# Up projections of the last ConvFFN in Strassen's form for the second token half, with pw2 put ahead of a down group

## The chip, the cores and the metric

One Trainium2 chip, one NeuronCore of it. The metric is the device time of one launch in microseconds. The engines are PE (matmul; its weight loads are listed as PEld), DVE (elementwise, reads SBUF and PSUM), ACT (activations and copies), POOL (elementwise, SBUF alone) and SP (issues DMAs). Each engine works through its own queue in order.

## The reference, cut to what matters

A decoder trunk of two layers runs over 16 meta tokens, 1024 prompt tokens and 8 samples of 4 tokens (1072 in all), with 1024 features in float32. Layer 0 mixes with an S5 scan and a short convolution, layer 1 with a Conformer convolution module; behind each stands a ConvFFN. The change lies in layer 1:

```
x = x + silu(layer_norm(dwconv31(v))) @ w_pw2 + b_pw2        # end of the mixer
xn = rms_norm(x) * g                                         # one factor per token
a, g = split(xn @ w_up)                                      # 2 x 2816 features
x = x + (silu(dwconv3(a)) * g) @ w_down
y = rms_norm(x) * g_final
```

`dwconv3` is causal over the tokens of the prompt and of each sample, and its last inputs are outputs too.

## The kernel before

Features lie on the 128 partitions, tokens along a row. The 1072 tokens are two halves: half 0 has 512 (in layer 1 only 496 or 498 of them are computed, since the meta tokens' results are not wanted), half 1 has 560 (528 of the prompt and 32 of the samples) and runs in two blocks of 280 columns. A residual tile `x` (`xres`) of 128 features by one half stays in SBUF: eight for each half.

Every float32 product is made of three in the `fp32r` type: both operands are split into a high part (`wh`, `xnh`, `hh`: a copy by ACT) and a rest (`wl`, `xnl`, `hl`: a subtraction, on DVE or POOL), and PE adds up high x high, high x rest and rest x high in a PSUM bank (L143, in `dense`). A weight tile of 128x1024 comes by DMA into one of two `raw` buffers (L110), and its parts go into a ring of three `wh`/`wl` pairs. POOL takes the subtraction for a share of the weights, DVE for the others (`weight`).

ConvFFN: 22 tiles `f` of 128 features. `up(f, hf)` computes tile `a` (8 K tiles x 3 parts x 2 blocks = 48 matmuls in half 1), multiplies it by the norm's factor `rstd` while it leaves PSUM (`ap`), runs the convolution over it (`c`: one step on ACT, two on DVE), then computes tile `g` in the same way; `s = silu(c) * g` (POOL) is split into `hh` and `hl`. `down(fs, ...)` multiplies a group of 4 tiles (one group has 2) with `w_down` and adds the result to the eight `x`. `run` takes the groups in turn, with the first up of the next group ahead of each down. Because `rstd` is applied at the eviction, the up matmuls don't wait for the norm.

The norm: squares of `x` are added up over the tiles (ACT and POOL), PE sums over the partitions (`nrm`, L222), DVE takes three Newton steps (`nrs`, L230 to L239), PE spreads the result over the partitions (`bcs`, L251), and ACT copies it out (`rstd`, L260). The layer norm of the Conformer module uses the same helper; its convolution of 31 taps over half 1 (`cva`, `cvb`) is spread by a tick count over the ups and downs of half 0 in layer 1.

The program's order is made by a scheduler: it takes the instructions in the order of the code as their priority and places each on its engine by a timing model. So the order of the code sets it, but not alone. In layer 1 the code has: all ups and downs of half 0; the rest of the convolution and the layer norm of half 1; `pw2` of half 1 (8 x 48 matmuls, with `b_pw2` added and the tiles `xn` split for the next ups, L161); the norm of half 1; the output of half 0 (L1011 and POOL); ups and downs of half 1, and the last norm and output (`finals`), whose order is written out by hand.

Of the kernel before, what the change touches and what calls it, by code (L numbers as in the profile page):

```python
# [67 lines left out]
def build(nc, tc, ctx, a):  # L68
# [704 lines left out]
    class FFN:  # L773
        def __init__(self, layer, xs, rs, dead=0):

            self.layer, self.xs, self.rs, self.dead = layer, xs, rs, dead
# [4 lines left out]
            self.fout = sm.tile([P, FT, NS + 1, 2], F32, tag="fout", name="fout")
            self.carry = sm.tile([P, FT, 2], F32, tag="carry", name="carry")

        def up(self, f, hf, tag, htag="t"):
# [46 lines left out]

        def run(self, hf, tag, done=None, tail=None):
            groups = GROUPS if tail else GROUPS[1:2] + GROUPS[:1] + GROUPS[2:]
            hs = [self.up(f, hf, tag) for f in groups[0]]
# [97 lines left out]
    def lnorm(cts, total, out, hf):  # L932
        mus = slot("xh", "mus", hf)
        for t0, n in BLK[hf]:
            b = bank("mu")
            PE.matmul(b[:, :n], ones, total[:, t0:t0 + n], start=True, stop=True)
            A.activation(mus[:, t0:t0 + n], b[:, :n], AF.Copy)
        acc = None
        for i in range(KT):
            tt(cts[i], cts[i], mus, SUB)  # L940
            sq = slot("xh", "sq", hf)
            A.activation(sq, cts[i], AF.Square)
            if acc is None:
# [8 lines left out]
        for i in range(KT):
            tt(cts[i], cts[i], lr, MUL)
            A.activation(cts[i], cts[i], AF.Silu, scale=lng[:, i:i + 1], bias=lnb[:, i:i + 1])
            out.append(cts[i])
            yield
# [144 lines left out]


# [86 lines left out]
```

## Time and profile before

| | |
|---|---|
| median of 3 runs | 2247.02 us (2246.21 to 2248.82) |
| the profiled execution | 2249.03 us, its span 2247.2 us, mean granted clock 0.994 |
| last down of half 0, layer 1 | from 1743.9 us on, 21.6 us |
| pw2 of half 1 | from 1765.5 us on, 49.6 us |
| ups and downs of half 1, layer 1 | from 1815.0 us to about 2205 us |
| matmuls | 13758, of them 2112 in the ups of half 1, layer 1 |

The profile is of one execution. A row of the time line gives the start and length in us, engine, line, operation, what is written and read, the shape and a count; the brackets at its end give the idle time before it and who ended that. Neighbours on an engine overlap a little in these rows, so the spacing of starts is what one instruction costs in a row of them. A matmul's row shows a modelled length; there too the spacing counts.

### The profile page before, as it was taken

To read this page: it belongs to the slowest core of one execution; us is meant where nothing else is said; L and a number is where in the kernel's file an instruction comes from. 1 tells how busy PE (TensorE), PEld (TensorE's weight loads), DVE (VectorE), ACT (ScalarE), POOL (GpSimd) and SP (SyncE) were. 2 spreads that over 40 slices of the span, in tenths; PEclk is the share of its full clock that TensorE was granted. 3 is DMA by queue.
4 is the path that set the end of the run, shared out by engine and by line. 5 is a ranking of instruction groups with operands and counts; after the bars stand their busy time and mean duration, and the time that the engine had idled before them with its cause. 6 is when DMAs were issued, how large, how long until landed. Compare 5 with 4: busy or idle time off the path is not lost.

```text
span 2247.2 us, 34396 instructions
## 1 busy us (share of the span) xinstructions
PE 2208.3 (98%) x13758; PEld 2009.0 (89%) x13758; DVE 1615.4 (72%) x2601; ACT 764.3 (34%) x1051; POOL 836.2 (37%) x684
## 2 busy tenths in 40 slices
PE   7999999999999999999999999999999999999997
PEld 6888898888888889999999998878888999999997
DVE  8979966545544678888896789799988566456554
ACT  5122354322332423232243423333334433223232
POOL 3212114323333434333443436455454543233241
PEclk8999999999999999999999999999999999999999
DMA  5334541333333332222223354333333332222231
GB/s 169 93 97 130 189 137 54 94 94 94 94 94 94 94 94 86 86 83 85 85 83 95 85 108 99 94 94 91 106 91 90 101 112 85 85 86 85 85 94 64
DMA packets 98336, 218.08 MB, mean 97 GB/s; under 512 B 28416, under 2 KB 45184, under 8 KB 98176
## 3 DMA queue, kind: packets, MB, share of 16 engines
q1 hardware_dynamic: 97632, 215.37, 32.8%
q8 instruction: 108, 1.77, 0.3%
q10 hardware_dynamic: 544, 0.52, 0.1%
q14 instruction: 52, 0.43, 0.1%
HBM read 202.49 MB, written 13.36 MB: 96 GB/s over the span
## 4 chain that ended last, share of the span: by engine, by line
PE 86%; DVE 10%; ACT 1%; DMA 1%; issue 1%; POOL 0%; SPq 0%; POOLq 0%; DVEq 0%; ACTq 0%
PE mm L143 83%; DVE c L497 1%; DVE xr L101 1%; DMA x<-x 1%; DVE cva L897 1%; DVE cvb L897 1%; DVE xnl L161 1%; PE bcs L251 1%; DVE wl L101 1%; DVE sq L101 1%; DVE hl L101 1%; DVE sg L101 0%; ACT wh L113 0%; PE nrm L222 0%; PE s L441 0%
## 5 line engine op out<-in xcount | busy, mean ns | idle before, releaser
L143 PE MATMUL mm<-xnh,wh 128*128 128x280 f32 (+3 forms) x2880 | 788.8, 326 | 6.6 <-ACT xnh L160 6.6
L143 PE MATMUL mm<-xnl,wh 128*128 128x280 f32 (+3 forms) x2880 | 790.8, 326 | 3.6 <-DVE xnl L161 3.6
L143 PE MATMUL mm<-xnh,wl 128*128 128x280 f32 (+3 forms) x2880 | 789.6, 326 | 0.0
L101 POOL TENSOR_TENSOR wl<-raw,wh 128x1024 fp32r<-128x1024 f32 x203 | 498.9, 2458 | 645.9 <-ACT wh L113 629.4
L113 ACT ACTIVATE wh<-raw 128x1024 fp32r<-128x1024 f32 x344 | 364.7, 1060 | 770.7 <-PE mm L143 681.7
L143 PEld LDWEIGHTS mm<-xnh,wh 128*128 128x128 f32 x2880 | 489.4, 189 | 47.2 <-ACT xnh L160 6.6
L143 PEld LDWEIGHTS mm<-xnl,wh 128*128 128x128 f32 x2880 | 488.8, 188 | 47.1 <-DVE xnl L161 5.5
L143 PEld LDWEIGHTS mm<-xnh,wl 128*128 128x128 f32 x2880 | 488.4, 188 | 40.1 <-issue 0.8
L143 PE MATMUL mm<-hh,wh 128*128 128x280 f32 (+2 forms) x992 | 284.4, 328 | 5.7 <-DVE xr L101 5.7
L143 PE MATMUL mm<-hl,wh 128*128 128x280 f32 (+2 forms) x992 | 284.7, 327 | 0.7 <-DVE hl L101 0.6
L143 PE MATMUL mm<-hh,wl 128*128 128x280 f32 (+2 forms) x992 | 283.6, 327 | 0.0
L101 DVE TENSOR_TENSOR xr<-mm,xr 128x280 f32<-128x280 f32 (+4 forms) x336 | 166.6, 522 | 159.4 <-PE mm L143 159.0
L497 DVE SCALAR_TENSOR_TENSOR c<-ap,fw,c 128x576 f32<-128x576 f32 (+2 forms) x176 | 212.6, 1208 | 46.8 <-ACT c L495 43.9
L101 POOL TENSOR_TENSOR s<-s,g 128x560 f32<-128x560 f32 (+2 forms) x88 | 132.6, 1506 | 281.8 <-DVE g L101 196.9
L101 DVE TENSOR_TENSOR wl<-raw,wh 128x1024 fp32r<-128x1024 f32 x141 | 192.0, 1361 | 31.8 <-ACT wh L113 30.4
L143 PEld LDWEIGHTS mm<-hh,wh 128*128 128x128 f32 x992 | 172.6, 189 | 22.0 <-DVE xr L101 7.7
L143 PEld LDWEIGHTS mm<-hl,wh 128*128 128x128 f32 x992 | 172.5, 188 | 15.7 <-DVE hl L101 1.3
L143 PEld LDWEIGHTS mm<-hh,wl 128*128 128x128 f32 x992 | 171.8, 188 | 14.4
L897 DVE SCALAR_TENSOR_TENSOR cvb<-vp,w_dw,cvb 128x512 f32<-128x512 f32 x240 | 179.8, 750 | 0.0
L897 DVE SCALAR_TENSOR_TENSOR cva<-vp,w_dw,cva 128x512 f32<-128x512 f32 x240 | 179.7, 749 | 0.1
L101 DVE TENSOR_TENSOR ap<-mm,rstd 128x32 f32<-128x32 f32 (+3 forms) x176 | 68.3, 429 | 126.2 <-PE mm L143 114.0
L101 DVE TENSOR_TENSOR hl<-s,hh 128x560 fp32r<-128x560 f32 (+2 forms) x88 | 101.0, 1148 | 51.8 <-ACT hh L157 51.7
(219 smaller groups left out, 2087.0 us busy)
## 6 DMA issues: line engine op xcount, KB each, us to landing
raw<-w_up SPq DMA_DIRECT2D x176, 512.0 KB
raw<-w_down SPq DMA_DIRECT2D x88, 512.0 KB
raw<-w_pw SPq DMA_DIRECT2D x48, 512.0 KB
raw<-w_in SPq DMA_DIRECT2D x22, 512.0 KB
raw<-w_out SPq DMA_DIRECT2D x12, 512.0 KB
du<-up SPq DMA_DIRECT2D x8, 292.0 KB
u<-du SPq DMA_DIRECT2D x32, 73.0 KB
x<-x SPq DMA_DIRECT2D x8, 280.0 KB
```

Source lines behind the costliest of these rows:

```text
L101: return e.tensor_tensor(o, x, y, op=op)
L113: A.activation(h, raw, AF.Copy)
L143: PE.matmul(banks[b][:, :n_], wl if i == 2 else wh, xx[:, t0:t0 + n_], start=(k == 0 and i == 0), stop=(k == n - 1 and i == 2))
L161: V.scalar_tensor_tensor(l, src, scale, h.bitcast(F32), op0=MUL, op1=SUB)
L251: PE.matmul(b[:, c * w:(c + 1) * w], one1[:w], dg[:, c0 + c], start=True, stop=True)
L497: mk = V.scalar_tensor_tensor(dst[:, :n], src[:, k:k + n], w[:, k:k + 1], dst[:, :n], op0=MUL, op1=ADD)
L897: V.scalar_tensor_tensor(b, v, w, b, op0=MUL, op1=ADD)
```

## The change

The ups of half 1 in layer 1 no longer use `up` but `up7`. The weights of an up are seen as a 2x2 matrix of blocks (rows: tile `a`, tile `g`; columns: the first and the second four K tiles), the tokens as another (rows: the K halves; columns: the first 280 and the last 280 tokens). With `A` the weights and `B` the tokens the seven products of half the K depth are

```
S1 = A21 + A22   S2 = S1 - A11   S3 = A11 - A21   S4 = A12 - S2
T1 = B12 - B11   T2 = B22 - T1   T3 = B22 - B12   N4 = B21 - T2
a, tokens   0..279: A11 B11 + A12 B21
a, tokens 280..559: A11 B11 + S2 T2 + S1 T1 + S4 B22
g, tokens 280..559: A11 B11 + S2 T2 + S3 T3 + S1 T1
g, tokens   0..279: A11 B11 + S2 T2 + S3 T3 + A22 N4
```

each of 4 K tiles x 3 parts of 280 columns, 12 matmuls: 84 for an up in place of 96. Sums that grow are kept in one bank (`bx`, `by`) and read on the way. The last product (`rest`) is put off into the next up or down (`flush`).

`prepare` builds the token operands once, with `rstd` and the norm's weight multiplied in, on DVE: per pair of tiles two scalings of 560 columns, four sums of 280, and three or four splits into `oh` (ACT) and `ol` (DVE). Per up, `up7` makes four weight sums and seven splits of 128x512; all subtractions of them and the product with `g` are on DVE (before: POOL had the product and half of the splits).

`between` puts the rest of half 1's convolution, its layer norm, `pw2`, the norm and `prepare` ahead of half 0's last down. `out0` puts the output of half 0 behind the first up of half 1. Twelve empty ticks in `lnorm` are gone.

On PE, at the next to last down of half 0 (`hh`, `hl`: its operands), before the change; `nrm` is the sum for half 1's layer norm:

```order
L143 MATMUL mm<-hh,wh 128x496
L143 MATMUL mm<-hl,wh 128x496
L143 MATMUL mm<-hh,wl 128x496
L222 MATMUL nrm<-ones,sq 112x1 x5
L143 MATMUL mm<-xnh,wh 128x498
L143 MATMUL mm<-xnl,wh 128x498
L143 MATMUL mm<-xnh,wl 128x498
```

The same instruction after the change:

```order
L143 MATMUL mm<-xnl,wh 128x496
L143 MATMUL mm<-xnh,wl 128x496
L143 MATMUL mm<-hh,wh 128x496
L143 MATMUL mm<-hl,wh 128x496
L143 MATMUL mm<-hh,wl 128x496
L143 MATMUL mm<-hh,wh 128x496
L143 MATMUL mm<-hl,wh 128x496
L222 MATMUL nrm<-ones,sq 112x1 x5
L143 MATMUL mm<-hh,wl 128x496
```

It stood behind the last of the down's 96 matmuls and now stands behind the fifth.

On PE, at the end of `pw2` (`csh`, `csl`) before the change:

```order
L143 MATMUL mm<-csh,wh 128x280 x2
L143 MATMUL mm<-csl,wh 128x280 x2
L143 MATMUL mm<-csh,wl 128x280 x2
L143 MATMUL mm<-xnh,wh 128x280 x2
L143 MATMUL mm<-xnl,wh 128x280 x2
```

After the change `pw2` is followed by half 0's last down, with `nrm` of half 1's norm behind its 41st matmul and `bcs` behind its 83rd. Its end, and the first products of half 1 (`oh`, `ol`):

```order
L143 MATMUL mm<-hh,wl 128x496
L143 MATMUL mm<-hh,wh 128x496
L143 MATMUL mm<-hl,wh 128x496
L143 MATMUL mm<-hh,wl 128x496
L893 MATMUL mm<-oh,wh 128x280
L893 MATMUL mm<-ol,wh 128x280
L893 MATMUL mm<-oh,wl 128x280
L222 MATMUL nrm<-ones,sq 124x1 x4
L893 MATMUL mm<-oh,wh 128x280
```

Where the ups of half 1 came straight behind `pw2`, the down stands between them. The second `nrm` is that of half 0's output.

On DVE after the change, behind the Newton steps of half 1's norm (`dg` is what `bcs` spreads); `xa`, `xb` and the two numbered `x` are the operands that `prepare` builds, `a22l` belongs to the first up's weights:

```order
L239 SCALAR_TENSOR_TENSOR nrs<-nrs 112x5
L101 TENSOR_TENSOR dg<-ident,nrs 112x560
L101 TENSOR_TENSOR xr<-mm,xr 128x496 x3
L836 SCALAR_TENSOR_TENSOR xa<-xr,gam,rstd 128x560
L836 SCALAR_TENSOR_TENSOR xb<-xr,gam,rstd 128x560
L101 TENSOR_TENSOR xr<-mm,xr 128x496
L101 TENSOR_TENSOR x_16811<-xb,xa 128x280
L101 TENSOR_TENSOR xa<-xa 128x280
L101 TENSOR_TENSOR x_16811<-xb,xa 128x280
L101 TENSOR_TENSOR x_16814<-xb,x_16811 128x280
L836 SCALAR_TENSOR_TENSOR xa<-xr,gam,rstd 128x560
L836 SCALAR_TENSOR_TENSOR xb<-xr,gam,rstd 128x560
```

Before, `pw2`'s evictions were followed by the splits into `xnl` one by one (L161), without `rstd`; now the scalings stand behind the norm. The diff, without the shortest parts:

```diff
+        def prepare(self, xr, gi, r):
+            self.ops = {n: [] for n in ("B11", "B21", "B22", "T1", "T2", "T3", "N4")}
+            H = self.H = TN[1] // 2
+            def hl(t, *names):
+                h, l = slot("xh", "oh", 1, F32R), slot("xh", "ol", 1, F32R)
+                A.activation(h, t, AF.Copy)
+                tt(l, t, h.bitcast(F32), SUB)
+                for i, n in enumerate(names):
+                    self.ops[n].append((h[:, i * H:(i + 1) * H], l[:, i * H:(i + 1) * H]))
+            for k in range(KT // 2):
+                xa, xb, x2 = [slot("v", n, 1) for n in ("xa", "xb", "x2")]
+                for o, i in ((xa, k), (xb, k + KT // 2)):
+                    V.scalar_tensor_tensor(o, xr[i][1], gam[:, gi, i:i + 1], r, op0=MUL, op1=MUL)
+                if k % 2 == 0:
+                    x4 = slot("v", "x4", 1)
+                (p, q), (b21, b22) = [(t[:, :H], t[:, H:]) for t in (xa, xb)]
+                t2, t3 = x2[:, :H], x2[:, H:]
+                tt(t3, b22, q, SUB)
+                tt(q, q, p, SUB)
+                tt(t2, b22, q, SUB)
+                tt(x4[:, k % 2 * H:(k % 2 + 1) * H], b21, t2, SUB)
+                hl(xa, "B11", "T1")
+                hl(xb, "B21", "B22")
+                hl(x2, "T2", "T3")
+                if k % 2:
+                    hl(x4, "N4", "N4")
+        def up7(self, f, tag, htag, stag, atag):
...
+            (a11, a12), (a21, a22) = [(t[:, :M], t[:, M:]) for t in raws]
+            w11, w12 = halves(ring())
+            hl(w11, a11)
+            s1, s2, s3, s4 = [slot(stag, "s%d" % i, [P, M]) for i in range(1, 5)]
+            tt(s1, a21, a22, ADD)
+            ws1, ws2 = halves(ring())
+            hl(ws1, s1)
+            hl(w12, a12)
+            tt(s2, s1, a11, SUB)
+            hl(ws2, s2)
+            tt(s4, a12, s2, SUB)
+            ws4, ws3 = halves(ring())
+            hl(ws4, s4)
+            tt(s3, a11, a21, SUB)
+            hl(ws3, s3)
+            w22 = hl([slot(atag, "a22" + c, [P, M], F32R) for c in "hl"], a22)
+            def product(b, w, x, start):
+                for k, xk in enumerate(self.ops[x]):
+                    for i in range(3):
+                        PE.matmul(b[:, :H], w[i == 2][:, k * P:(k + 1) * P], xk[i == 1],
...
+            product(bx, w11, "B11", True)
+            A.activation(ap[:, 2:2 + H], bx[:, :H], AF.Copy)
+            product(by, ws1, "T1", True)
+            A.activation(g, by[:, :H], AF.Copy)
+            product(bz, w12, "B21", True)
+            tt(ap[:, 2:2 + H], ap[:, 2:2 + H], bz[:, :H], ADD)
+            product(bx, ws2, "T2", False)
...
+            product(by, ws4, "B22", False)
+            tt(sp, sp, by[:, :m], ADD)
+            tt(sa, sa, sj(by, m), ADD)
...
+            self.flush()
+            product(bx, ws3, "T3", False)
+            tt(g, g, bx[:, :H], ADD)
+            tt(s[:, H:], s[:, H:], g, MUL)
+            def rest():
+                product(bx, w22, "N4", False)
+                tt(s[:, :H], s[:, :H], bx[:, :H], MUL)
+                h[1] = split(s, "h", 1, tag=htag)
+            self.pend = rest
...
             def get(m):
+                if m == 1:
+                    self.flush()
...
+                if hook and not tail and not more:
+                    hook()
                 self.down(fs, hs, hf, *((None, None) if more else (done, tail)))
...
-        if hf:
-            for _ in range(12):
-                yield
         lr = inv_std(acc, "xh")
...
-    f1.run(0, "t", last(0, META, TN[0] - META))
-    drain(conv1)
-    fills.clear()
-    pw2(1, csB, done2)
-    rs2[1] = nm2.rstd(1)
-    r = fin[0, META].rstd(0)
-    out(0, META, TN[0] - META, r, r)
-    f1.run(1, "v", None, finals)
+    def between():
+        drain(conv1)
+        fills.clear()
+        pw2(1, csB, lambda m, x, hf: nm2.add(x, hf))
+        f1.prepare(xres, 3, nm2.rstd(1))
+    def out0():
+        r = fin[0, META].rstd(0)
+        out(0, META, TN[0] - META, r, r)
+    f1.run(0, "t", last(0, META, TN[0] - META), None, between)
+    f1.run(1, "v", None, finals, out0)
```

More of the change, by code (lines that the diff above doesn't have):

```diff
@@ L782, in __init__ @@
             self.carry = sm.tile([P, FT, 2], F32, tag="carry", name="carry")
+            self.pend = None
         def up(self, f, hf, tag, htag="t"):
@@ L816, in up @@
             return {hf: split(s, "h", hf, tag=htag, t0=d)}
+        def prepare(self, xr, gi, r):
+            self.ops = {n: [] for n in ("B11", "B21", "B22", "T1", "T2", "T3", "N4")}
+            self.pend = None
+            H = self.H = TN[1] // 2
[22 more added lines that the diff above has]
+                    hl(x4, "N4", "N4")
@@ new lines, in up7, with ring, hl, halves @@
+        def up7(self, f, tag, htag, stag, atag):
+            fw, n, H = self.fw[:, f], ntok(1), self.H
+            o, M = 2 + n, P * KT // 2
+            raws = []
+            for i in range(2):
+                raw = wp.tile([P, 1024], F32, tag="raw", name="raw", bufs=2)
+                SY.dma_start(raw, a["w_up"][(self.layer * FT + f) * 2 + i])
+                raws.append(raw)
+            def ring():
+                return [wp.tile([P, 1024], F32R, tag=t, name=t, bufs=WB) for t in ("wh", "wl")]
+            def hl(hl_, raw):
+                A.activation(hl_[0], raw, AF.Copy)
+                tt(hl_[1], raw, hl_[0].bitcast(F32), SUB)
+                return hl_
+            def halves(w):
+                return [[t[:, i * M:(i + 1) * M] for t in w] for i in range(2)]
+            (a11, a12), (a21, a22) = [(t[:, :M], t[:, M:]) for t in raws]
[18 more added lines that the diff above has]
+                        PE.matmul(b[:, :H], w[i == 2][:, k * P:(k + 1) * P], xk[i == 1],
+                                  start=(start and k == 0 and i == 0), stop=(k == KT // 2 - 1 and i == 2),
+                                  skip_group_check=True)
+            bx, by, bz = [bank("mm", "mm") for _ in range(3)]
+            ap = slot(tag, "ap", [P, o + 6 * NS])
+            PL.tensor_copy(ap[:, 0:2], self.carry[:, f])
+            PL.tensor_copy(s6(ap, o)[:, :, 0:2], self.fin[:, f])
+            g = slot("t", "g", [P, H])
+            product(bx, w11, "B11", True)
[5 more added lines that the diff above has]
+            product(bx, ws2, "T2", False)
+            m = n - H
+            sa, sp = s6(ap, o)[:, :, 2:6], ap[:, 2 + H:o]
+            A.activation(sp, bx[:, :m], AF.Copy)
+            A.activation(sa, sj(bx, m), AF.Copy)
+            product(by, ws4, "B22", False)
+            tt(sp, sp, by[:, :m], ADD)
+            tt(sa, sa, sj(by, m), ADD)
+            PL.tensor_copy(self.fout[:, f], last2(ap, o))
+            nc_ = n + 6 * NS
+            c = slot(tag, "c", [P, nc_ + 2])
+            conv3(c, ap, fw, nc_)
+            s = slot("t", "s", 1)
+            A.activation(s[:, :n], c[:, :n], AF.Silu)
+            A.activation(sj(s), s6(c, o)[:, :, 0:4], AF.Silu)
+            self.flush()
+            product(bx, ws3, "T3", False)
+            tt(g, g, bx[:, :H], ADD)
+            tt(s[:, H:], s[:, H:], g, MUL)
+            h = {}
+            def rest():
[3 more added lines that the diff above has]
+            self.pend = rest
+            return h
@@ L818, in down, with flush @@
+        def flush(self):
+            p, self.pend = self.pend, None
+            if p:
+                p()
         def down(self, fs, hs, hf, done, tail=None):
@@ L830, in down, with run, up @@
             residual(get, done, xres, (hf,), blk=((d, TN[0] - d),) if d else None)
-        def run(self, hf, tag, done=None, tail=None):
+        def run(self, hf, tag, done=None, tail=None, hook=None):
             groups = GROUPS if tail else GROUPS[1:2] + GROUPS[:1] + GROUPS[2:]
-            hs = [self.up(f, hf, tag) for f in groups[0]]
+            def up(f):
+                if not tail:
+                    return self.up(f, hf, tag)
+                i = f - GROUPS[-1][0]
+                h = self.up7(f, tag, "xh" if i in (0, 1) else "v" if i > 1 else "t",
+                             *(("v", "t") if f < 3 else ("x", "x")))
+                if f == 0:
+                    hook()
+                return h
+            hs = [up(f) for f in groups[0]]
             for i, fs in enumerate(groups):
@@ L837, in run @@
                 early = len(more) if tail and i + 2 == len(groups) else 1
-                nxt = [self.up(f, hf, tag, "xh" if early > 1 else "t") for f in more[:early]]
+                nxt = [up(f) for f in more[:early]]
+                if hook and not tail and not more:
+                    hook()
                 self.down(fs, hs, hf, *((None, None) if more else (done, tail)))
-                hs = nxt + [self.up(f, hf, tag) for f in more[early:]]
+                hs = nxt + [up(f) for f in more[early:]]
         def finish(self):
```

## The prediction

> **What bounds the kernel now.** I read the page first (busy shares, the chain that ended last), then the busy time by stage, then the time lines of the engines around the places that the change touches.
>
> ```profile
> PE 2208.3 (98%) x13758; PEld 2009.0 (89%) x13758; DVE 1615.4 (72%) x2601; ACT 764.3 (34%) x1051; POOL 836.2 (37%) x684
> PE 86%; DVE 10%; ACT 1%; DMA 1%; issue 1%; POOL 0%; SPq 0%; POOLq 0%; DVEq 0%; ACTq 0%
> 1510.00:1690.00 180.00, 179.36 (x798) 149.39 (x796) 165.68 (x223) 61.24 (x80) 88.87 (x56) 1.00 0.31 93
> 1690.00:1720.00 30.00, 30.00 (x144) 25.38 (x145) 20.36 (x32) 8.69 (x10) 14.41 (x8) 1.00 0.35 106
> 1720.00:1822.00 102.00, 102.00 (x644) 94.50 (x643) 61.38 (x70) 50.51 (x70) 50.05 (x27) 1.00 0.31 93
> 1822.00:1862.00 40.00, 38.53 (x301) 37.86 (x300) 32.73 (x60) 13.05 (x21) 17.45 (x17) 1.00 0.36 118
> 1960.00:2060.00 100.00, 100.00 (x777) 100.00 (x776) 57.83 (x74) 30.51 (x41) 31.65 (x32) 1.00 0.29 85
> ```
>
> The window rows give length, then PE, weight loads, DVE, ACT, POOL (busy us and instructions), and the granted clock. PE is the bound everywhere that the change reaches; from 1690 on it hardly rests. DVE has no room before 1690 (165.7 of 180 us) and over 40% to spare in the up and down stage after 1862. So matmuls removed there are time saved, as long as DVE keeps up with what replaces them.
>
> **What is removed.** In 1960 to 2060, 777 matmuls of 280 columns took 100 us: 0.1287 us each. An up has 96 of them now and 7 x 12 = 84 after; 22 ups make 264 fewer: **-34.0 us**. [...]
>
> **First cost: the layer norm's inverse, moved ahead.** Its sums over the partitions (`nrm`) stood behind all 96 matmuls of the next to last down; they now stand behind the fifth, and `bcs` 40 matmuls further on. The same place before:
>
> ```profile
> 1687.99 0.38 PE L143 MATMUL mm<-hh,wl 128*128 128x496 f32 x1
> 1689.91 0.49 PE L143 MATMUL mm<-hl,wh 128*128 128x496 f32 x1 [0.64 <-DVE hl L101]
> 1690.35 0.73 DVE L101 TENSOR_TENSOR sq<-sq 128x560 f32<-128x560 f32 x1
> 1692.14 1.50 DVE L497 SCALAR_TENSOR_TENSOR c<-ap,fw,c 128x496 f32<-128x496 f32 x2
> 1696.43 2.21 DVE L101 TENSOR_TENSOR hl<-s,hh 128x496 fp32r<-128x496 f32 x1 [1.62 <-ACT hh L157]
> 1695.70 5.21 POOL L101 TENSOR_TENSOR wl<-raw,wh 128x1024 fp32r<-128x1024 f32 x2
> ```
>
> The sum that `nrm` reads is ready at 1691.1 (the `sq` row's end); PE would reach `nrm` at 1688.0 and waits 3.1 us, of which 0.6 was lost anyway. Behind it the Newton steps stand in DVE's queue behind `c` and around this `hl` (which waits for ACT), while POOL splits weights. They end near 1704, and PE reaches `bcs` at 1692.0 + 40 x 0.2246 = 1701.0: another 2.5 to 3 us. I take **+5.0** (3 to 7).
>
> **Second cost, the large one: the new operands.** Today the up of half 1 begins before the rms norm is known, because its factor is applied at the eviction. The new sums mix tokens of different factors, so `prepare` has to put the factor into the operands: every product waits for the norm, and then for DVE. The cover is the last down of half 0:
>
> ```profile
> 1743.91 0.39 PE L143 MATMUL mm<-hh,wh 128*128 128x496 f32 x1
> 1765.47 0.42 PE L143 MATMUL mm<-csh,wh 128*128 128x280 f32 x2
> 1815.02 0.42 PE L143 MATMUL mm<-xnh,wh 128*128 128x280 f32 x2
> 1821.74 0.89 PE nrm L222 x10
> 1828.93 1.10 PE bcs L251 x10
> 1832.75 0.76 PE nrm L222 x8
> 1840.82 0.89 PE bcs L251 x8
> 1829.85 0.70 ACT L260 ACTIVATE rstd<-bcs 128x448 f32<-128x448 f32 x2 [0.41 <-PE bcs L251]
> ```
>
> (The four short rows are of the chain that ended last: half 1's norm, then half 0's.) The down's 96 matmuls take 1765.47 - 1743.91 = 21.6 us (0.2246 each). Count from its first one. `nrm` comes behind 41 (9.2 us), takes 0.9, `bcs` behind 42 more (19.5 us), takes 1.1, and ACT's two copies bring `rstd` at 21.5 us. PE is through with the down at 21.6 + 2.0 = 23.6 us. DVE's durations, from rows where nothing disturbs it; its instructions overlap by some 0.1 us, so I use the spacing of neighbours:
>
> ```profile
> 1727.94 1.38 DVE L101 TENSOR_TENSOR csl<-cv,csh 128x560 fp32r<-128x560 f32 x2
> 1817.25 0.79 DVE L161 SCALAR_TENSOR_TENSOR xnl<-xr,gam,xnh 128x560 fp32r<-128x560 f32 x1
> 1863.54 1.51 DVE L101 TENSOR_TENSOR xr<-mm,xr 128x280 f32<-128x280 f32 x4
> L101 DVE TENSOR_TENSOR kl<-raw,kh 128x512 fp32r<-128x512 f32 x4 | 2.7, 690 | 3.9 <-ACT kh L128 3.9
> 1833.63 0.81 DVE L497 SCALAR_TENSOR_TENSOR c<-ap,fw,c 128x576 f32<-128x576 f32 x1
> 1826.38 0.17 DVE L239 SCALAR_TENSOR_TENSOR nrs<-nrs 112x5 f32<-112x5 f32 x1
> ```
>
> That is 0.65 us for 560 columns, 0.69 for the scaling, 0.36 for 280, 0.60 for 512, 0.73 for a conv step, 0.2 for a Newton step. From `rstd` to the end of the operands DVE has 8 scalings (5.5), 16 sums of 280 (5.8), 14 splits of 560 (9.1), 9 instructions of 512 for the first up's weights (5.4), a residual and ten Newton steps of half 0's norm (2.6): 28.4 us. PE can't finish its first product before most of it is done, because `k = 3` comes last. Up to the third up's eviction of `bz` DVE then has 21 of 512 (12.6), 8 of 280 (2.9), four conv steps (2.9), the six scalings of half 0's output (3.8) and smaller ones (2.2): 24.4 us. Together **53 us, in which PE has 84 + 84 + 36 = 204 matmuls, 26.3 us.** So PE falls behind by (21.5 + 53 + 0.7 for the last eviction) - (23.6 + 26.3) = 25.3 us, plus whatever holds DVE up:
>
> ```profile
> 1878.13 2.40 POOL L101 TENSOR_TENSOR wl<-raw,wh 128x1024 fp32r<-128x1024 f32 x1
> 1878.51 3.50 DVE L497 SCALAR_TENSOR_TENSOR c<-ap,fw,c 128x576 f32<-128x576 f32 x2 [0.85 <-ACT c L495]
> 1877.72 0.20 POOL L800 COPY fout<-ap 128x18 f32<-128x18 f32 x1 [9.68 <-DVE ap L101]
> 1764.95 4.80 POOL L101 TENSOR_TENSOR sq<-sq 128x496 f32<-128x496 f32 x3
> 1842.41 2.91 POOL L101 TENSOR_TENSOR xr<-xr,rstd 128x496 f32<-128x496 f32 x2 [1.82 <-ACT rstd L260]
> ```
>
> Two conv steps are 1.5 us of work and took 3.5, ending 1.5 us after POOL's 2.4 us instruction: a DVE instruction with two SBUF operands waits for POOL's to end. In the 53 us POOL has two or three of the 1.6 us sums, the two output scalings (2.9), eight copies (1.6) and perhaps one split (2.4): about 9.5 us, of which I let 8 count (3 to 12). **+33.3.** Half 0's own `nrm` and `bcs` (x8: 0.76 and 0.89 us of PE today) fall into this wait: **-1.7.**
>
> **Steady ups and downs.** By the rows between two evictions of `bz`, DVE has 8.4, 10.0 and 9.4 us for three ups of a group and 22.7 for the one that holds the down. PE takes 10.8 and 35.6. What comes on top per up is 0.6 us of POOL's copies and a wait for the second `raw`: it is requested when `a22l` is done and needed 3.0 us later, and takes
>
> ```profile
> 1698.13 6.36 SPq L110 DMA_DIRECT2D raw<-w_up  x3
> 1701.82 1.06 ACT L113 ACTIVATE wh<-raw 128x1024 fp32r<-128x1024 f32 x1 [4.47 <-DMA raw<-w_up]
> ```
>
> 3.7 us from issue to use, so 0.9 us of wait. DVE gets up to 11.5 against 10.8 and is late by 1 to 2 us at a group's end; the down gives it back. PE needs `w11` of the next up only 38 matmuls (4.9 us) after `bz`, and it takes 1.6 us, so 3.3 us of lateness costs nothing. ACT's share grows from 30 to some 60 of 100 us (seven splits of 0.6 us in place of two of 1.06, and four copies) and bounds nothing. What moves on the queues: SP asks for `pw2`'s eight weights ahead of the down's, and for half 0's output after two ups; nearly all of SP's waits are for a `raw` to come free, DMA is busy 0.3 of the time, and I put that at nothing (if it isn't hidden, 3.7 us once). I take **+1.0**, for the seven ups in a row of the last two groups (0 to 5).
>
> **The clock.**
>
> ```profile
> 1500.00:1505.00 5.00, 4.19 (x19) 3.18 (x17) 4.96 (x8) 2.13 (x4) 0.00 (x0) 1.00 0.24 58
> 1505.00:1510.00 5.00, 3.99 (x11) 3.26 (x12) 5.00 (x9) 1.25 (x2) 3.59 (x2) 0.66 0.38 122
> 40.00:50.00 10.00, 6.47 (x30) 6.41 (x31) 8.11 (x30) 1.01 (x2) 0.00 (x0) 0.50 0.17 52
> ```
>
> PE rested 1.8 us in these first ten, and the granted clock was 0.66 over the second five, 1.7 us lost; while PE was busy only 6.5 of 10 us it stayed at 0.50. The wait for the operands is longer than both. Most of the slow matmuls hide behind DVE: **+2.5** (1 to 8).
>
> **Sum:** -34.0 + 5.0 + 33.3 - 1.7 + 1.0 + 2.5 = +6.1 us. The profiled execution took 2249.0 (span 2247.2 and 1.8 around it), so 2255.1; the median of the runs is 2.0 lower, so **2253**.
>
> **Rivals.**
> 1. *DVE is held up little, and it ends faster.* If POOL's instructions fall into DVE's own waits (none of the 8 us), the norm costs 3.0, and the chain of 53 us runs in 50, the loss is 22.3 in place of 33.3: -34 + 3 + 22.3 - 1.7 + 1 + 1 = -8.4, so 2239. It decides below about 28 us of loss. For it: evictions from PSUM are not held, as the first of the rows below shows inside the second. Against: nearly all of `prepare` reads SBUF twice. 0.17.
>
> ```profile
> 1866.89 0.45 DVE L101 TENSOR_TENSOR xr<-mm,xr 128x280 f32<-128x280 f32 x1 [0.32 <-PE mm L143]
> 1865.64 2.40 POOL L101 TENSOR_TENSOR wl<-raw,wh 128x1024 fp32r<-128x1024 f32 x1 [5.18 <-ACT wh L113]
> ```
>
> 2. *DVE or the weight buffers bound the steady ups.* Should the wait for `raw` be 2 us, an up takes DVE 12.6 us; past 3.3 us of lateness PE loses 1 us an up, some 17 us in all: 2270. For it: all 11 weight instructions of an up are on DVE now, and three `wh`/`wl` pairs are all used by one up. Against: the down's 13 us of room. 0.13.
> 3. *The clock stays low through the whole of the operands.* 26.3 us of matmuls become 52.6 beside DVE's 61, and DVE's evictions wait for them: +8 more, 2261. [...] 0.06.
> 4. *The operands are hidden after all*, and little but 8 us of cost remains: 2221. Against it stands the whole sum of DVE. 0.04.
>
> **How the numbers follow.** The forecast has 0.60, from 2245 to 2263; +-0.2% (4.5 us: 2242.5 to 2251.5), about what a measurement of this kernel tells from no change, takes 0.26 of it and slower 0.34. Of rival 1, 0.11 is faster and 0.06 within. Rivals 2 and 3 are slower (0.19), rival 4 faster (0.04). Together: faster 0.15, same 0.32, slower 0.53. The range takes in the low norm and collision bounds (-34 + 3 + 28.3 - 1.7 + 0 + 1 = -3.4, 2243.6) and, upward, most of the high ones (-34 + 7 + 37.3 - 1.7 + 5 + 8 = +21.6, 2268.6): 2242 to 2267.
>
> **What would show it.** PE idle near 3 us twice around 1690 to 1705. About 20 us between the last matmul of half 0's down and an unbroken run of products, with DVE busy throughout and named as the releaser. Slices of 0.5 clock there. 84 matmuls in 10.8 us an up later, and PE full. A wait on DVE inside the later ups would speak for rival 2; PE idle under 15 us at the operands for rival 1.

## The result, and the profile after

The changed kernel took 2260.47 us (median of 6 runs, 2258.40 to 2262.50), the kernel before 2248.76 us beside it (6 runs, 2246.21 to 2249.48). The ratio is **1.0054, 95% interval 1.0041 to 1.0067**: slower, by 11.7 us. The profiled execution took 2259.5 us (span 2257.7), 10.5 more than that of before. Forecast were 2253, +6.1 us, and a range of 2242 to 2267: the time is in the range, and the change nearly twice the one forecast.

The page of the changed kernel, busy times and the chain that ended last:

```profile
PE 2187.5 (97%) x13494; PEld 1984.0 (88%) x13494; DVE 1705.0 (76%) x2875; ACT 829.5 (37%) x1255; POOL 745.0 (33%) x638
PE 82%; DVE 10%; issue 3%; DMA 2%; ACT 2%; POOL 1%; SPq 0%; POOLq 0%; ACTq 0%; DVEq 0%
```

PE has 13758 - 13494 = 264 matmuls less, as it should, and is busy for 20.8 us less in a span that is 10.5 longer. So it rests some 31 us more. The windows show where (length, PE, weight loads, DVE, ACT, POOL, clock, as before):

```profile
1690.00:1700.00 10.00, 9.65 (x36) 8.26 (x37) 9.69 (x20) 3.63 (x5) 3.93 (x3) 0.67 0.32 99
1797.90:1821.00 23.10, 23.10 (x115) 19.64 (x115) 10.33 (x26) 6.20 (x11) 4.39 (x3) 1.00 0.17 46
1821.00:1846.90 25.90, 6.65 (x22) 4.47 (x20) 25.80 (x43) 11.07 (x20) 9.13 (x7) 0.60 0.00 0
1846.90:1866.00 19.10, 18.43 (x128) 17.98 (x129) 18.59 (x40) 11.61 (x24) 5.06 (x5) 0.91 0.25 84
1866.00:1886.10 20.10, 12.81 (x73) 12.32 (x72) 16.52 (x27) 7.09 (x15) 3.37 (x5) 0.79 0.38 131
1886.10:1910.00 23.90, 21.27 (x154) 20.38 (x153) 17.75 (x36) 8.38 (x16) 4.39 (x4) 0.97 0.37 130
1821.00:1886.10 65.10, 37.89 (x219) 34.76 (x218) 60.90 (x107) 29.77 (x57) 17.56 (x17) 0.75 0.19 65
1920.00:2150.00 230.00, 230.00 (x1788) 230.00 (x1787) 184.78 (x341) 115.27 (x228) 25.13 (x48) 1.00 0.29 92
```

There are two stalls. The first, 1821 to 1847, is the one that was forecast: DVE is busy 25.8 of 25.9 us and PE has 22 matmuls. The second, 1866 to 1887, was not: PE is idle 7.3 us, and the granted clock is 0.79 from 1866 to 1886. From 1910 on PE is full, 1788 matmuls in 230 us, 0.1286 each.

To compare runs I use two marks on PE, the first matmul of `pw2` and the first of the tail (`kh`, the last down). Of before (first row; its `pw2` began at 1765.47), the changed kernel, and at the end the layer norm's two PE steps:

```profile
2204.87 0.31 PE L143 MATMUL mm<-hh,kh 128*128 128x308 f32 x1
...
1748.31 0.42 PE L143 MATMUL mm<-csh,wh 128*128 128x280 f32 x2
2215.73 0.30 PE L143 MATMUL mm<-hh,kh 128*128 128x308 f32 x1
...
1690.35 2.02 PE L222 MATMUL nrm<-ones,sq 128*112 128x1 f32 x10 [3.04 <-DVE sq L101]
1703.30 1.26 PE L251 MATMUL bcs<-dg,one 112*128 112x112 f32 x10
```

Up to `pw2` the changed kernel is 1748.31 - (1765.47 - 21.56) = 4.4 us behind. From there to the tail it takes 467.4 us against 439.4 + 21.6 = 461.0, so 6.5 more. `nrm` waits 3.04 us, as forecast. `bcs` does not wait; instead the clock was 0.67 for the ten microseconds between them, a loss of 3.3 us.

The beginning of the first stall on DVE, then what ACT and POOL did there:

```profile
1820.98 1.25 DVE L836 SCALAR_TENSOR_TENSOR xa<-xr,gam,rstd 128x560 f32<-128x560 f32 x1 [1.11 <-ACT rstd L260]
1822.15 1.77 DVE L836 SCALAR_TENSOR_TENSOR xb<-xr,gam,rstd 128x560 f32<-128x560 f32 x1
1823.84 0.66 DVE L101 TENSOR_TENSOR xr<-mm,xr 128x496 f32<-128x496 f32 x1
1826.75 1.37 DVE L101 TENSOR_TENSOR x<-xb,xa 128x280 f32<-128x280 f32 x1
1831.12 0.79 DVE L836 SCALAR_TENSOR_TENSOR xb<-xr,gam,rstd 128x560 f32<-128x560 f32 x1
1819.17 1.62 ACT L200 ACTIVATE sq<-xr 128x496 f32<-128x496 f32 x3
1820.70 0.25 ACT L260 ACTIVATE rstd<-bcs 128x112 f32<-128x112 f32 x1
1820.36 10.23 POOL L101 TENSOR_TENSOR sq<-sq 128x496 f32<-128x496 f32 x7 [17.52 <-ACT sq L200]
```

`rstd` is complete only at 1820.95, 23.0 us behind the down's first matmul (1797.96), since three squares of half 0 stand between its two copies on ACT. Then POOL's seven sums run in one piece beside `prepare`: a scaling takes 1.77 us in place of 0.79 (the last DVE row, behind POOL's end), a sum of 280 columns 1.37 in place of 0.44 (1833.08). The instruction from PSUM in between takes 0.66, and the same one 0.68 at 1815.36, ahead of the sums.

The second stall: DVE, SP's queue, and the two waits on PE.

```profile
1867.48 6.08 DVE L1148 SCALAR_TENSOR_TENSOR xr<-xr,gam,rstd 128x496 f32<-128x496 f32 x6 [0.80 <-ACT rstd L260]
1873.48 0.68 DVE L101 TENSOR_TENSOR a22l<-raw,a22h 128x512 fp32r<-128x512 f32 x1
1874.19 0.50 SPq L859 DMA_DIRECT2D raw<-w_up  x1
1880.17 0.69 DVE L101 TENSOR_TENSOR s<-raw 128x512 f32<-128x512 f32 x1 [1.13 <-DMA raw<-w_up]
1874.58 0.60 PE L893 MATMUL mm<-oh,a22h 128*128 128x280 f32 x1 [3.39 <-DVE g L101]
1881.58 0.60 PE L893 MATMUL mm<-oh,wh 128*128 128x280 f32 x1 [3.90 <-ACT wh L866]
```

Six scalings of half 0's output stand ahead of `a22l`, the last reader of a `raw` buffer. When it is done (1874.16) the next weight is requested (1874.19), and PE waits twice: for an eviction behind the six, and for the weight.

### The profile page after: what moved, and what is told of

Read it like the earlier page. It is cut to its first block, busy times and chain, and to the rows that moved or that the text cites. A ratio compares the mean times of both kernels' runs of the same rounds, so it can differ in the third digit from the quotient of the medians.

```text
span 2257.7 us, 34330 instructions
## 1 busy us (share of the span) xinstructions
PE 2187.5 (97%) x13494; PEld 1984.0 (88%) x13494; DVE 1705.0 (76%) x2875; ACT 829.5 (37%) x1255; POOL 745.0 (33%) x638
## 4 chain that ended last, share of the span: by engine, by line
PE 82%; DVE 10%; issue 3%; DMA 2%; ACT 2%; POOL 1%; SPq 0%; POOLq 0%; ACTq 0%; DVEq 0%
PE mm L143 70%; PE mm L893 10%; DVE c L497 1%; DVE xr L101 1%; DVE cva L1037 1%; DVE cvb L1037 1%; DVE xnl L161 1%; PE bcs L251 1%; DMA raw<-w_up 1%; DVE hl L101 1%; DVE wl L101 1%; DVE sq L101 1%; ACT wh L113 1%; DMA raw<-w_down 0%; DMA raw<-w_in 0%
## 5 line engine op out<-in xcount | busy, mean ns | idle before, releaser
L143 PE MATMUL mm<-xnh,wh 128*128 128x280 f32 (+3 forms) x2176 | 637.4, 337 | 6.9 <-ACT xnh L160 6.9
L143 PE MATMUL mm<-xnl,wh 128*128 128x280 f32 (+3 forms) x2176 | 640.0, 338 | 2.3 <-DVE xnl L161 2.3
L143 PE MATMUL mm<-xnh,wl 128*128 128x280 f32 (+3 forms) x2176 | 638.4, 337 | 0.0
L143 PEld LDWEIGHTS mm<-xnh,wh 128*128 128x128 f32 x2176 | 376.1, 188 | 47.2 <-ACT xnh L160 6.9
L143 PEld LDWEIGHTS mm<-xnl,wh 128*128 128x128 f32 x2176 | 375.8, 188 | 45.7 <-DVE xnl L161 4.0
L143 PEld LDWEIGHTS mm<-xnh,wl 128*128 128x128 f32 x2176 | 376.2, 189 | 40.3 <-issue 0.8
L101 DVE TENSOR_TENSOR wl<-raw,wh 128x1024 fp32r<-128x1024 f32 (+1 forms) x165 | 181.5, 1110 | 23.0 <-ACT wh L113 19.3
L893 PE MATMUL mm<-oh,wh 128*128 128x280 f32 x528 | 156.6, 298 | 16.0 <-ACT oh L828 8.3
L893 PE MATMUL mm<-ol,wh 128*128 128x280 f32 x528 | 156.3, 297 | 8.8 <-DVE ol L101 8.8
L101 POOL TENSOR_TENSOR s<-s,g 128x512 f32<-128x512 f32 (+2 forms) x66 | 90.5, 1371 | 214.0 <-DVE g L101 182.1
```

Of the source, the lines that this page charges most:

```text
L101: return e.tensor_tensor(o, x, y, op=op)
L143: PE.matmul(banks[b][:, :n_], wl if i == 2 else wh, xx[:, t0:t0 + n_], start=(k == 0 and i == 0), stop=(k == n - 1 and i == 2))
L893: PE.matmul(b[:, :H], w[i == 2][:, k * P:(k + 1) * P], xk[i == 1], start=(start and k == 0 and i == 0), stop=(k == KT // 2 - 1 and i == 2) ...
```

## The experiments

The kernel before ran beside each group of runs (its median 2247.3 to 2247.8 us). "Over before" is the difference of medians there; the changed kernel's own is +11.7. "Stage" is the time from `pw2` to the tail by the two marks. "Loss" is the stage less what PE needs: the 458.99 us of the run with the old ups in the new order, where PE waited for nothing from `pw2` to the tail, less 12 x 0.1287 = 1.544 us for each up by seven products. Both are read from one execution of each run, and executions of the changed kernel spread over 4.1 us: a difference of a few us in them says little alone.

| run | ratio to before, 95% | over before, us | `pw2` begins | stage | loss |
|---|---|---|---|---|---|
| changed kernel | 1.0054 (1.0041 to 1.0067) | +11.7 | 1748.3 | 467.4 | 42.4 |
| e1_ticks_back | 1.0013 (1.0004 to 1.0022) | +3.2 | 1742.6 | 463.6 | 38.5 |
| e2_move_alone | 1.0016 (1.0007 to 1.0024) | +3.5 | 1747.3 | 459.0 | 0 |
| e3_no_factor | 0.9986 (0.9977 to 0.9995) | -4.3 | 1747.2 | 451.6 | 26.6 |
| e4_out0_later | 1.0037 (1.0024 to 1.0049) | +7.7 | 1746.4 | 464.8 | 39.8 |
| e5_squares_later | 1.0082 (1.0069 to 1.0096) | +18.6 | 1747.6 | 475.1 | 50.0 |
| r3_three_raw | 1.0080 (1.0066 to 1.0094) | +18.0 | 1749.4 | 470.8 | 45.8 |
| o2_two_old_ups | 0.9948 (0.9935 to 0.9960) | -11.4 | 1741.0 | 449.7 | 21.5 |
| o4_four_old_ups | 0.9952 (0.9939 to 0.9964) | -10.9 | 1742.6 | 450.4 | 19.2 |
| x1_no_half0_norm | 0.9984 (0.9975 to 0.9993) | -3.4 | 1747.6 | 452.3 | 27.3 |
| q0_output_in_pieces | 1.0051 (1.0039 to 1.0064) | +11.5 | 1746.0 | 469.8 | 44.8 |
| q4_pieces_everywhere | 0.9945 (0.9932 to 0.9959) | -13.0 | 1741.9 | 446.1 | 14.9 |
| z0_pieces_three_raw | 1.0071 (1.0057 to 1.0085) | +16.1 | 1747.6 | 470.8 | 45.8 |

### The moves apart from the products

e1 gives the layer norm its twelve empty ticks back:

```diff
             yield
+        if hf:
+            for _ in range(12):
+                yield
         lr = inv_std(acc, "xh")
```

> The twelve empty ticks are put back into the layer norm of half 1, so its nrm stands again behind all 96 matmuls of the next-to-last down; nothing else is changed. If the term 'layer norm's inverse moved ahead' is real (the wait of 3.04 us at nrm and the slow clock behind it, 0.67 from 1690 to 1700), the time falls by 3 to 5 us, to about 2256, and PE does not wait at nrm. Rival: the later nrm only pushes the wait on to the first matmul of pw2 (110 matmuls, 25 us behind bcs in place of 196) and the time stays within 1 us of the changed kernel's 2260.

e2 keeps the moves and takes the old `up`:

```diff
-                h = self.up7(f, tag, "xh" if i in (0, 1) else "v" if i > 1 else "t", ...)
+                h = self.up(f, hf, tag, "xh" if i >= 0 else "t")
...
-        pw2(1, csB, lambda m, x, hf: nm2.add(x, hf))
-        f1.prepare(xres, 3, nm2.rstd(1))
+        pw2(1, csB, done2)
+        rs2[1] = nm2.rstd(1)
```

> The moves of the change without its products: pw2, the norm and the output of half 0 stand where the change puts them, and half 1's ups are the old ones with eight half products (unscaled operands, factor at the eviction). If the moves cost only the layer norm's inverse (+4), less half 0's nrm and bcs and the wait for the norm, the time is 2250 to 2254 against 2248.8 before. If SP's moved requests cost something of their own, it is 2256 or more. If the moves are free, 2248 to 2249.

`nrm` in e1, then the first matmul of `pw2` in e1 and in e2:

```profile
1708.10 1.05 PE L222 MATMUL nrm<-ones,sq 128*112 128x1 f32 x10
1742.60 0.42 PE L143 MATMUL mm<-csh,wh 128*128 128x280 f32 x2
1747.27 0.43 PE L143 MATMUL mm<-csh,wh 128*128 128x280 f32 x2
```

In e1 `nrm` takes 1.05 us without a wait, in place of 3.04 + 2.02. Over the four runs of this study with the ticks, `pw2` begins at 1742.0 in the mean; over the seven with two `raw` buffers and without the ticks (the changed kernel among them), at 1747.2. So that step costs **5.2 us**; it was put at 5.0. e1 gained more than I expected (8.5 us by the medians). Of the profiled pair's gain 5.7 us lie ahead of `pw2` and 3.9 behind it, where its edit does not reach, and I have no cause for those. e2 is in its expected interval: the moves cost 3.5 us net, so **the seven products themselves cost 8.3 us** (+11.7 against +3.5), a saving of 34.0 and a loss of 42.4.

### Is the loss the wait for the norm?

```diff
-                    V.scalar_tensor_tensor(o, xr[i][1], gam[:, gi, i:i + 1], r, op0=MUL, op1=MUL)
+                    V.tensor_scalar(o, xr[i][1], gam[:, gi, i:i + 1], None, op0=MUL)
```

> The operands are made without the norm's factor (rstd is left out of them and nothing multiplies it in later), so prepare can begin while pw2 still runs; same matmuls, the same number of instructions on DVE. My theory, that the loss at the operands comes from the wait for the norm with DVE's chain behind it: PE runs from the down into the products with under 5 us of idle time, no slow clock there, and the time falls by 25 to 33 us, to 2227 to 2235 (what is left of the saving is then the layer norm's 4 and the wait for raw in the third up). Rival, that DVE's amount of work and POOL's collisions count wherever they stand: less than 12 us, above 2248.

```profile
1790.00:1820.00 30.00, 30.00 (x165) 26.20 (x164) 29.83 (x51) 13.29 (x21) 7.91 (x6) 1.00 0.21 67
1820.00:1850.00 30.00, 25.09 (x178) 23.96 (x177) 21.37 (x50) 15.13 (x33) 11.08 (x10) 0.94 0.18 53
1850.00:1870.00 20.00, 10.26 (x50) 9.51 (x49) 16.06 (x25) 6.85 (x13) 3.33 (x5) 0.66 0.40 137
```

(Windows of e3.) It gained 16.0 us, between my 25 to 33 and the rival's 12, so **my theory holds for 16 us of the loss and falls for the 26.6 that stay**. (The edit also makes the eight scalings another instruction; how much of the 16.0 is theirs, this run doesn't show.) `prepare` now runs beside `pw2` and the down (DVE 29.83 of 30 us), and the first stall is nearly gone (4.9 us idle). But the second is there in full: 9.7 us idle, clock 0.66. The same six scalings stand in it (6.04 us, from 1851.16 on), so it doesn't come from the wait for the norm of half 1.

### The second stall: scalings, squares, buffers

e4 puts half 0's output behind the third up in the code; e5 issues half 0's squares together with the output; r3 has three `raw` buffers and one buffer less of tag `t`.

```diff
 e4
-                if f == 0:
+                if f == 2:
                     hook()
 e5
-            nm.add(x, hf)
-            if m % 3 == 2:
-                A.activation(x, x, AF.Copy, scale=gam[:, 4, m:m + 1])
+            late.append((m, x, hf))
...
+        for m, x, hf in late:
+            fin[0, META].add(x, hf)
...
         r = fin[0, META].rstd(0)
 r3
-NXT, NXH, NTT, NVT = 16, 32, 15, 8
+NXT, NXH, NTT, NVT = 16, 32, 14, 8
...
-        raw = wp.tile([P, 1024], F32, tag="raw", name="raw", bufs=2)
+        raw = wp.tile([P, 1024], F32, tag="raw", name="raw", bufs=3)
```

> The output of half 0 (six scalings on DVE, two on POOL, eight stores) stands behind the third up of half 1 in the code in place of the first. In the changed kernel the six took 6.08 us ahead of a22l of the second up, whose end (1874.16) let the next raw load go (1874.19). My theory, that this queue on DVE is what holds the third up: 5 to 8 us less, 2252 to 2255. Rival, that DVE has the same sum to do and only the place changes: within 2 us of 2260.

> The squares and sums of half 0's x (POOL's seven instructions, 10.23 us in one piece from 1820.36 in the changed kernel) are issued with the output of half 0, behind the first up of half 1; the results are the same. In the changed kernel they ran beside the first instructions of prepare, whose DVE rows stretched from 0.65 to between 0.9 and 1.8 us, some 6 us lost. If that collision is on the path: 4 to 7 us less, 2253 to 2256. Rival, that the sums only collide with DVE a little later, where it is as late: within 2 us of 2260.

> Three raw buffers in place of two (one buffer of another pool, tag t, is given up for them), in the whole program. In the changed kernel the third up's second weight was requested only when a22l of the second up was done (1874.19) and PE stood or ran at a low clock from 1871 to 1890. If the wait for a raw buffer is what makes that stall: 5 to 8 us less, 2252 to 2255, and no wait on a DMA of w_up there. Rival, that the six output scalings ahead of it on DVE hold the products directly (a22l and the weights are late whatever has been loaded): 0 to 3 us less.

e4 gained 4.0 us (expected 5 to 8; its interval overlaps the changed kernel's): the six scalings now stand among the first down's evictions, and PE waits there, 3.2 us for `xr`. e5 missed both what I expected and the rival. It shows that the collision with POOL is real (48 DVE instructions in the 25.8 us of the first stall, 43 in the changed kernel), and that moving it away in this manner pays nothing. Its windows:

```profile
1821.00:1846.90 25.90, 12.04 (x56) 9.85 (x56) 25.80 (x48) 12.48 (x24) 6.10 (x2) 0.67 0.12 41
1850.00:1890.00 40.00, 24.43 (x135) 22.94 (x134) 26.31 (x50) 16.17 (x33) 12.86 (x12) 0.71 0.22 77
```

In the first stall PE is busy 12.04 us in place of 6.65: 5.4 us won. But half 0's sums and norm now fall between the first ups, where PE waits for them (1.9 us at `nrm`, 3.0 at `bcs`), and between 1850 and 1890 it is idle 15.6 us: 6.9 us slower in all. r3 is 6.3 us slower, too, outside both forecasts. In its second stall the wait for the weight is gone, and the one for the eviction behind the six scalings stands, with 4.40 us: so a third `raw` buffer takes one of the two waits away and doesn't pay. Why it costs time I can't say; it changes the order of the whole program.

### Cover: the first ups in the old form

o2 and o4 compute the first two or four ups of half 1 from unscaled operands, as before, so that they need not wait for the norm. `prepare` is split: `B11`, `T1`, `B21`, `B22` first, then the others, computed in place. The ticks are back.

```diff
+                if f < 4:                      # o4; 2 in o2
+                    h = self.up(f, hf, "t")
+                else:
+                    h = self.up7(...)
+                if f == 0:
+                    self.second = prep()
+                if f == 3:                     # o4; 1 in o2
+                    self.second()
...
             def second():
                 for k in range(KT // 2):
...
                     tt(t1, b22, t1, SUB)       # T2 = B22 - T1
                     tt(p, t1, p, SUB)          # T3 = T2 - B11
                     hl(xa, "T3", "T2")
```

> Ticks back as in the run with that name, and the first two ups of half 1 by eight half products from unscaled operands (no wait for the norm); prepare (its sums in two parts, the second behind the first 16 operands) has these two ups to hide behind, and half 0's output stands behind the second. Twenty ups by seven products: 31 us saved. The loss between pw2 and the end that is 42.4 us in the changed kernel and 38.6 with the ticks back should fall by the 24.7 us of cover, to 10 to 20: 2230 to 2240, faster than before. Rival, from the run without the factor (26.6 left when the operands wait for nothing): the ramp of the first seven-product ups costs 20 to 27 wherever it stands: 2240 to 2246.

> As the run before with four ups by eight half products: 27.8 us saved, and two more ups and a down of cover. Loss 3 to 10: 2224 to 2232, if the loss is DVE's backlog behind the norm and goes with cover. Rival, that the ramp of the first seven-product ups costs 20 us or more wherever it stands: 2240 to 2247.

Both are **faster than before by 0.5%**. o2 is within my interval; but its loss is 21.5, the rival's size, and o4 misses: twice the cover took only 2.3 us off the loss and cost 3.1. So some 20 us did not go with more cover of the norm.

### Taking work from DVE, and only moving it

x1 leaves out half 0's last norm and the scaling of its output by it:

```diff
-            nm.add(x, hf)
...
-            if m % 3 == 2:
-                tt(x, x, r, MUL, PL)
-            else:
-                V.scalar_tensor_tensor(x, x, gam[:, 4, m:m + 1], b, op0=MUL, op1=MUL)
...
-        r = fin[0, META].rstd(0)
```

> The last norm of half 0 and the scaling of its output by it are left out (no squares and sums, no Newton steps, no scalings; the stores stay, and half 0's output is unscaled). It takes from the ramp POOL's 10.2 us of sums and 2.9 us of scalings, DVE's 6.1 us of scalings and some 2.5 us of small steps, and PE's 1.7 us. My present theory: the loss is DVE's, in two stalls; the first (1821 to 1847) shrinks by about 5 us as POOL's sums no longer hold prepare up (so it was when the squares were issued later), the second (1866 to 1910, 10 us idle and 4 of low clock) goes. 15 to 20 us less than the changed kernel: 2239 to 2245. Rival, that the ramp is bound by each up's own weight work on DVE and its loads: only the 5 us, 2253 to 2256.

```profile
1821.00:1846.90 25.90, 12.03 (x55) 9.77 (x55) 25.80 (x48) 12.68 (x24) 6.09 (x2) 0.67 0.14 51
1866.00:1886.10 20.10, 14.72 (x98) 14.00 (x97) 15.74 (x28) 9.17 (x17) 2.87 (x4) 0.92 0.33 105
1886.10:1910.00 23.90, 23.90 (x188) 23.90 (x187) 19.62 (x40) 10.98 (x23) 0.46 (x3) 1.00 0.29 89
```

15.1 us less, both by the medians and by the loss, within my interval. What was taken from DVE comes to nearly that: 5.4 us beside POOL's sums, 6.1 of scalings, and some 2 of Newton steps and `dg`. But PE's 1.7 us of sums and spreading and ACT's eight squares are gone with it, so x1 doesn't isolate DVE. Of the second stall one long wait is left, 4.38 us for an `hh` on ACT, at 1880.15. PE is full from 1886 (188 matmuls in 23.9 us, 154 in the changed kernel).

q0 keeps all of that work and puts the output in three pieces, each held behind the convolution of the third, fourth and fifth up. It also puts the end of half 0's norm behind the second up in the code, and the weight sums of the fourth and fifth up into other buffers. z0 is q0 with three `raw` buffers and two buffers less of tag `t`. q4 is o4 with such pieces, and with each `k` of `prepare` held behind an eviction or a convolution of the old ups (`AT` stands for the list of these places).

```diff
+        with tc.issue_after(f1.marks[f][0].ins):
+            out(0, META, TN[0] - META, r0, r0, PIECES.get(f, ()))
...
+            for k in range(KT // 2):           # q4
+                with tc.issue_after(self.marks[AT[k][0]][AT[k][1]].ins):
+                    first(k)
```

> The changed kernel with the output of half 0 in three pieces, each held behind the convolution of one of the third to fifth ups, so that no more than two scalings stand together in DVE's queue; nothing else is changed. If the second stall is the six scalings standing ahead of a22l and the products' weights: PE's idle time between 1866 and 1910 falls under 3 us, its clock stays at 1.00, and the time falls by 8 to 12 us, to 2247 to 2252. Rival, that the same DVE work hurts wherever it stands in the ramp (as with the output moved behind the third up in one piece): 3 to 5 us, 2255 to 2257.

> The run with the output of half 0 in pieces, with three raw buffers in place of two (two buffers of tag t given up). In that run the second stall was gone (PE idle 3.5 us from 1866 to 1910), yet PE stood again from 1920 to 1960 (6 us idle, and a low clock behind), and the time did not fall. There each load of w_up went out the moment a raw came free (1925.33, behind s3 of the up before, which the scalings had put back), and DVE waited 15 us for loads in ten ups. If this loop of two buffers (load 3.7 us, then DVE's sums, then the next load) is what gives the gain back: the later stalls go and the time is 2248 to 2254. Rival, that DVE is full there and its backlog comes out at the next down whatever is loaded: within 3 us of 2259.

> The run with four old ups, with each k of prepare held behind the convolution or the eviction of one of these ups, and the output of half 0 in pieces behind the sixth to eighth up. There PE waited in the old ups for evictions (g 3.9 us, xr 3.3, s 1.6, ap 0.9) that stood in DVE's queue behind prepare and the six scalings. If DVE has room enough there and only the order in its queue was bad, these waits go: the loss falls from 19 to between 5 and 11 us, 2223 to 2229. Rival, that DVE is full in that stretch whatever its order: 2233 or more.

q0 missed: PE's idle time between 1866 and 1910 fell from 9.9 to 3.0 us, and yet the time is the same, because PE stood again further on: 6.0 us between 1920 and 1960. Two scalings of a piece, the longest of these later waits, and what stood ahead of it on DVE and POOL:

```profile
1922.68 1.38 DVE L1150 SCALAR_TENSOR_TENSOR xr<-xr,gam,r 128x496 f32<-128x496 f32 x2
1948.79 0.51 DVE L101 TENSOR_TENSOR ap<-ap,mm 128x248 f32<-128x248 f32 x2 [2.53 <-PE mm L895]
1949.85 2.37 POOL L101 TENSOR_TENSOR wl<-raw,wh 128x1024 fp32r<-128x1024 f32 x1
1950.47 3.21 DVE L497 SCALAR_TENSOR_TENSOR c<-ap,fw,c 128x576 f32<-128x576 f32 x2 [1.17 <-ACT c L495]
1954.90 0.60 PE L143 MATMUL mm<-hh,wh 128*128 128x280 f32 x1 [3.43 <-DVE s L101]
```

Ahead of this wait DVE itself waits 2.53 us for PE and 1.17 for ACT, and beside POOL's split (2.37 us) two steps of the convolution take 3.21 us, where one takes 0.81 with POOL at rest (1920.02): it is one up's chain from eviction to `s` that is late there, not a backlog of DVE. PE's products also stand in another order there than in the changed kernel; that this order makes the wait is a rival that no run tests.

I supposed the loop of two buffers (load, DVE's sums, next load) behind the later waits; z0 speaks against it: +16.1, slower even than the rival's interval. q4 (-13.0) has the lowest time of the study, **0.55% faster than before**, though its time is the rival's, not mine, and its interval overlaps those of o2 and o4. Two windows of q4, and one of o2 for the same stretch:

```profile
1830.00:1870.00 40.00, 37.25 (x285) 36.65 (x284) 39.71 (x72) 14.87 (x23) 18.19 (x14) 1.00 0.26 80
1870.00:1940.00 70.00, 63.32 (x477) 61.47 (x476) 55.35 (x98) 33.05 (x62) 14.70 (x17) 1.00 0.29 98
...
1830.00:1870.00 40.00, 29.82 (x201) 28.39 (x199) 38.64 (x71) 14.75 (x28) 14.03 (x12) 0.91 0.23 75
```

DVE is full in both (39.71 and 38.64 of 40). In q4 the evictions come first, so PE works 37.25 us beside it at a clock of 1.00; in o2 it works 29.82 at 0.91. Of the 10.7 us that PE still waits in q4, 6.7 lie between 1870 and 1940.

## Why the prediction was right, and where it was not

**The saving.** 264 matmuls at 0.1286 us: -34.0, as forecast.

**The layer norm's inverse.** Forecast +5.0, measured 5.2 by the runs with and without ticks (4.4 in the profiled pair). The first wait is there to 0.1 us. The second isn't; a clock of 0.67 behind the first took its place. The size was right by luck, with one of two mechanisms wrong.

**The operands: the term that was mis-sized.** Forecast were 33.3 - 1.7 for half 0's norm, and 3.5 for the steady part and the clock, 35.1. Measured against the stage before, as these terms are, it is 467.4 - 461.0 + 34.0 = 40.4. (The 42.4 of the table are 2.0 more, since e2's stage is that much shorter than the one before.) DVE's sum was right: 53 us and 8 of collisions, 61, from `rstd` to the third up's eviction of `bz`; that eviction ended at 1886.1, and DVE was busy for **60.9 us** of the way. The collisions were 5.6 us at the squares (the eight instructions up to 1831.12 took 10.1 us; in e5, without the sums beside them, 4.5) and some 2 at the output (six scalings in 6.08 us; q0's two take 1.38), 7.5 in all. What failed is the step that let DVE run through: it was idle 65.1 - 60.9 = **4.2 us** in between, five times for ACT or a weight (the 0.80 at `rstd` and 1.13 at `raw` above among them), and `rstd` came **1.5 us** late, 1.0 of it by the three squares on ACT (in e5 and x1, where they don't stand there, it came 22.0 us behind the down's first matmul). Then PE lost a further 23.9 - 154 x 0.1287 = 4.1 us up to 1910, about what clock and steady part were given. With 1.5 and 4.2 the stage's forecast of +1.1 becomes +6.8, and +6.5 was measured. The "3.7 us once" that I allowed for the moved loads and priced at nothing is part of that: the load of 1874.19, late behind the scalings, not behind SP's queue.

**What I said of hidden work.** "DVE has over 40% to spare" was true of the kernel before and not of the changed one. There DVE is busy 184.78 of 230 us, 80%. Its three longest waits in these 230 us (total, times, longest):

```profile
DVE s L101 <- DMA raw<-w_up: 21.8, 15, 3.1
DVE s L101 <- PE mm L893: 8.2, 6, 2.6
DVE ap L101 <- PE mm L893: 7.1, 6, 2.0
```

A wait for a load of `w_up` is 1.45 us in the mean, more than the 0.9 us an up that I had costed (and my own 3.7 less 3.0 gives only 0.7). Work taken from the ramp came back nearly one for one (x1), work only moved came back by 4 us at most (e4, q0) or cost time (e5), and a third buffer didn't help (r3, z0). I read this as a DVE that can't drain its backlog. No run isolates that, and the rows speak against it: from 1920 on DVE waits 18.5 us for PE in all, and already behind the second stall, at 1890.87, an eviction had waited 4.18 us for PE. Why moved work doesn't pay stays open.

**The rivals.** The first (little hold-up, faster) is out: PE's loss is 42 us, not under 28. The second is out as it was put, since PE never waits for DVE in the steady ups; its premise, that DVE is nearly full there, holds. The third (clock) did not decide: the clock was low through the first stall (0.60), as it said, but there PE had few matmuls and DVE was full. What the clock cost was at the second stall, 26 matmuls at a spacing of 0.233 us in place of 0.129, 2.7 us. No run isolates it.

## What to carry to other kernels

Saving matmuls by sums on another engine moved the bound here before it saved time (through the two stalls DVE was busy 60.9 of 65.1 us, PE 37.9): add up that engine's work from the first value that everything waits for to the point where it runs ahead again, with its own waits on loads and copies, and ask what share it then has left to catch up with. Cover for such a start is best made of work in the old form that doesn't need the late value; here two or four ups of 22, together with the layer norm's ticks, turned +0.5% into -0.5%. Of two ways to lighten the start, taking work away paid here and moving it mostly didn't.

## What the runs showed of the hardware

**DVE in step with POOL.** Through POOL's seven sums (10.23 us, 1.46 each), DVE's instructions with two SBUF operands went at about one to each, 0.89 to 1.77 us, whether they had 280 or 560 columns; where POOL rested, from 1831.12 on, the same forms took 0.44 with 280 columns and 0.79 with 560. The one from PSUM among them took 0.66, as without the sums (0.68). What in the chip ties the two engines together the rows don't show.

**The clock came back after 3.2 to 6.2 us.** After the first stall PE ran without a break from 1846.88 and its spacing fell from 0.233 to 0.129 us at 1850.1, 3.2 us on. After the second it took 6.0 us (from 1881.58 on), and behind the wait at `nrm` (1690.35) 6.2, where the spacing of 496 columns fell from 0.413 to 0.225:

```profile
1696.51 0.42 PE L143 MATMUL mm<-hh,wh 128*128 128x496 f32 x1
...
1846.88 0.60 PE L893 MATMUL mm<-oh,wh 128*128 128x280 f32 x1 [2.17 <-ACT wh L866]
1850.07 0.34 PE L893 MATMUL mm<-oh,wh 128*128 128x280 f32 x1
...
1887.58 0.35 PE L893 MATMUL mm<-ol,wh 128*128 128x280 f32 x1
1887.77 0.29 PE L893 MATMUL mm<-oh,wl 128*128 128x280 f32 x1
```

(The rows in which a matmul takes 0.42, 0.34 or 0.35 are the changes.) The waits just ahead of the three were 2.17, 3.90 and 3.04 us, so the longest of them did not have the longest return. Why the returns differ no run shows.
